# Two token blocks' last-phase work placed in TensorE's fixed order

## The chip, the cores and the metric

The kernel runs on one core of a Trainium2 chip. The core has TensorE (PE in the profile; the loads of its stationary operand are a row of their own, PEld), VectorE (DVE), ScalarE (ACT), GpSimd (POOL) and SyncE (SP), which here only issues DMAs. The metric is device time in microseconds (us), the median of several runs. Before the change it is 2971.01 us (three runs, 2964.57 to 2972.19).

## The reference

A decoder block over 2048 tokens of width 1024, in float32, with two mixers side by side; cut to its core:

```python
def _rwkv7_scan(r, decay, k, v, kk, b):
...
    def step(state, inp):
        r_t, w_t, k_t, v_t, kk_t, b_t = inp
        sk = jnp.einsum('bhvk,bhk->bhv', state, kk_t)
        state = (state * w_t[:, :, None, :] - sk[..., None] * b_t[:, :, None, :]
                 + v_t[..., None] * k_t[:, :, None, :])
        return state, jnp.einsum('bhvk,bhk->bhv', state, r_t)
...
def _conv_branch(val, gate, og, conv_k, conv_b, ln_g, ln_b, w_o):
    u = val * jax.nn.sigmoid(gate)
    u = _causal_depthwise_conv(u, conv_k, conv_b)
    u = _layernorm(u, ln_g, ln_b, LN_EPS)
    u = jax.nn.silu(u) * jax.nn.silu(og)
    return u @ w_o
...
        h = _rmsnorm(x, norm_g[l]) * (1.0 + scale[:, None, :]) + shift[:, None, :]
        p = jnp.einsum('bsd,de->bse', h, w_in[l])
        c_val, c_gate, c_og, ts, r_og, g_conv, g_rwkv = jnp.split(p, SPLITS, axis=-1)
...
        m = jax.nn.sigmoid(g_conv) * y_conv + jax.nn.sigmoid(g_rwkv) * y_rwkv
        out = jnp.einsum('bsd,de->bse', m, w_out[l])
        x = x + gate[:, None, :] * out
    return _rmsnorm(x, final_g)
```

The second mixer normalises the scan's output by head, adds a bonus term, gates it and multiplies it by w_rwkv_out. Its recurrence is the only part in which tokens depend on each other in a long row.

## The kernel before, in words

**Tiling.** Tokens go in four blocks of 512 (`TB`), b = 0 to 3; channels in eight tiles of 128 (`KT`). Every float32 product is made as three products of rounded parts (hi by hi, lo by hi, hi by lo; `mm3k`, L314), so a 128-channel output tile of a block takes 8 x 3 products of 512 columns. `msplit` cuts each in two of 256 columns in the first phase and leaves it at 512 in the last.

**First phase.** For each block 73 tiles of the input projection are made: K, R and V for the recurrence, value and gate for the convolution, one low-rank tile and four kinds of gates. Results that the last phase needs go to HBM: `o_d` (recurrence), `bv_d` (its bonus), `ro_d`, `co_d` (gates of the two mixers), `gr_d`, `gc_d` (merge gates), `y_d` (convolution). The recurrence is done in 16 groups G = 4b + g of four heads: `pair` (L582 on) makes chunk operands, `inverse` inverts a triangular matrix on GpSimd (31 dependent steps of two operations, L754 and L758), `merge` completes it on TensorE (L806, L816), and `group` walks a chain of eight steps of three small products each (L858, L864, L871), with a DVE operation between each two, then two products for the output (L885), a normalisation, and two transposes (L920) whose results are stored as `o_d`. Chain G needs chain G-1's end, and the K tiles of group G wait for chain G-2.

**TensorE's fixed order.** In the first phase the order on TensorE is written out by a small simulation, `compose`. Its clock counts only planned TensorE time (`te`). Threads (the steps of pair, group, inverse and merge, and background work) say after how much planned time they go on; between them jobs (a projected tile each, in pieces of one k) fill in. `pick` takes the first of the next `LOOK` = 13 jobs whose condition holds. `swap` exchanges the block's input tiles (`h_hi`, `h_lo`, eight buffers each) for those of the next block, which `hprep` loads and splits; `duo` interleaves two jobs so that the eight input tiles come free, or are first needed, one after the other. The other engines' orders and the DMA queue are made by a scheduler that knows priorities and data; each engine then runs its list in order. `behind` ties an operation to a place in TensorE's order.

**Background.** In blocks 1 and 2 a thread (`side`) splits the weights of the last phase into hi and lo and stores them, one item after another. In block 3 `z_thread` makes block 0's inputs for the last phase: `z_first` (o + bv) x ro, stored as `z_d`, and `lnorm_first`, the layer norm of `y_d` with its swish and gate, stored as `u_d`.

**Last phase.** After the fixed order is closed (`ctx_pe.__exit__`), for each block: `rproj` (eight tiles of w_rwkv_out, into `mr`), `cproj` (eight of w_conv_out, merged and split into `m_hi`, `m_lo`), the output product with w_out (`pout`, L1402 to L1404, 4 column blocks), the residual sum (L1410), the last RMS norm and the store (L1423). Block 0 takes `z_d` and `u_d` by `lsplit`. For the next block `osplit` (L1273, L1274 and the splits at L1251, L1252) and `lnorm` make the inputs while the output product runs. Their tiles lie where the first phase's lay: a pool can be used as soon as the tiles that were in its place are no longer needed. Block 0's tiles lie on the right side of the memory (`oa`), the next blocks' also on the left, where the chain's tiles were (`late`).

## Time and profile before

| what | us |
|---|---|
| median of three runs | 2971.01 |
| the profiled execution, device time | 2974.13 |
| its span (first to last record) | 2972.3 |
| span, until the first phase's projections end | about 2324 |
| span, the first output product begins | 2433.4 |
| span, the last product of the last chain (L885) begins | 2473.2 |

The profile is of one execution. Its page gives busy time by engine, the span in 40 slices, the chain of work that ended last, and groups of instructions by line of the kernel; the trace also answers for windows of time, for single tiles, for waits by engine and for lists of instructions in order of time. "Idle before <- releaser" names what the engine waited for last. The mean granted clock of TensorE was 0.974 over the span.

### The profile page before, as it was taken

The page shows a single profiled execution, that of the slowest core. Times are in us where ns is not written, and L with a number is a line of the kernel's source. Part 1 is how long each engine was busy: PE and PEld are TensorE (multiplying, and loading weights), DVE is VectorE, ACT ScalarE, POOL GpSimd, SP SyncE. Part 2 cuts the span into 40 slices and gives each one's busy share as a digit, 9 for nine tenths or more (in the row PEclk, how much of TensorE's full clock was granted, in tenths as well). Part 3 has the DMA queues.
Part 4 walks back from the last instruction along what each step waited for, and adds up shares of the span by engine and source line. Part 5 has one row for each costly group of instructions (what it writes and reads, how often), then busy time and mean ns, then how long its engine had stood idle before and what let it go on. Part 6 is the DMA issues. An engine that isn't in the chain of part 4 may idle for free.

```text
span 2972.3 us, 64197 instructions
## 1 busy us (share of the span) xinstructions
PE 2787.3 (94%) x25672; PEld 2625.0 (88%) x25672; DVE 2014.0 (68%) x3867; ACT 939.1 (32%) x1779; POOL 1273.5 (43%) x1790
## 2 busy tenths in 40 slices
PE   6998999899999999999999999999999995899998
PEld 6888989899999998999999889989999784687988
DVE  6695876767677685868595758686877443767333
ACT  4443334333333323332233232323333222333201
POOL 2456535742534352435334445466463424646000
PEclk9999999999999999999999999999999997999999
DMA  8776866766767675867667677666665765979684
GB/s 315 268 251 220 276 224 241 250 210 209 240 225 229 205 247 185 273 219 240 201 208 219 210 239 253 210 200 232 202 225 175 240 245 170 364 251 345 240 288 166
DMA packets 361548, 699.18 MB, mean 235 GB/s; under 512 B 129121, under 2 KB 147873, under 8 KB 361250
## 3 DMA queue, kind: packets, MB, share of 16 engines
q1 hardware_dynamic: 361250, 695.08, 69.6%
q8 instruction: 202, 3.31, 0.5%
q14 instruction: 96, 0.79, 0.1%
HBM read 506.14 MB, written 187.70 MB: 233 GB/s over the span
## 4 chain that ended last, share of the span: by engine, by line
PE 54%; DVE 18%; DMA 4%; issue 2%; POOL 1%; ACT 1%; SPq 0%; DVEq 0%; POOLq 0%; ACTq 0%
PE ps_main L314 40%; DVE acc L972 5%; PE xo L864 2%; PE xo L858 1%; PE xo L871 1%; PE pout L1402 1%; PE pout L1404 1%; PE pout L1403 1%; DVE uv L891 1%; PE aux L674 1%; DMA ct<-co_d 1%; DVE T L776 1%; DVE As L677 1%; DVE As L821 1%; DVE gst L910 1%
## 5 line engine op out<-in xcount | busy, mean ns | idle before, releaser
L314 PE MATMUL ps_main<-h_hi,w_hi 128*128 128x256 f32 x4608 | 968.0, 292 | 26.0 <-issue 13.8
L314 PE MATMUL ps_main<-h_hi,w_lo 128*128 128x256 f32 x4608 | 911.8, 280 | 3.5 <-POOL w_lo L293 3.0
L314 PE MATMUL ps_main<-h_lo,w_hi 128*128 128x256 f32 x4608 | 912.5, 280 | 0.0
L314 PEld LDWEIGHTS ps_main<-h_hi,w_hi 128*128 128x128 f32 x4608 | 708.6, 191 | 51.8 <-issue 16.5
L314 PEld LDWEIGHTS ps_main<-h_hi,w_lo 128*128 128x128 f32 x4608 | 706.1, 190 | 4.1 <-POOL w_lo L293 3.4
L972 DVE SCALAR_TENSOR_TENSOR acc<-u,ck,acc 128x512 f32<-128x512 f32 x928 | 696.7, 751 | 19.1
L314 PEld LDWEIGHTS ps_main<-h_lo,w_hi 128*128 128x128 f32 x4608 | 708.7, 190 | 0.0
L758 POOL TENSOR_TENSOR TT<-TT,itmp 128x126 f32<-128x126 f32 (+22 forms) x496 | 198.1, 399 | 35.4
L754 POOL TENSOR_TENSOR itmp<-La,TT 128x126 f32<-128x126 f32 (+22 forms) x496 | 187.7, 378 | 55.9 <-DMA La<-dA 21.0
L293 POOL TENSOR_TENSOR w_lo<-w_st,w_hi 128x1024 fp32r<-128x1024 f32 x51 | 123.7, 2426 | 183.8 <-ACT w_hi L291 157.0
L853 ACT ACTIVATE Se<-S,pe 128x128 f32<-128x128 f32 x256 | 89.0, 395 | 313.3 <-DVE S L875 311.8
L875 DVE TENSOR_TENSOR S<-xo,Se 64x128 f32<-64x128 f32 x256 | 73.6, 287 | 137.5 <-PE xo L871 133.0
L866 DVE TENSOR_TENSOR uv<-xo,rn 64x256 f32<-64x256 f32 x128 | 53.8, 421 | 126.6 <-PE xo L864 125.3
L291 ACT CAST w_hi<-w_st 128x1024 fp32r<-128x1024 f32 x71 | 74.5, 1050 | 193.7 <-DMA w_st<-w_in_t 158.6
L642 POOL TENSOR_TENSOR ta<-ta,k 128x512 f32<-128x512 f32 x32 | 45.1, 1411 | 176.5 <-ACT ta L641 176.5
L557 ACT ACTIVATE t<-ps_main,mu 128x512 f32<-128x512 f32 x96 | 65.8, 685 | 133.1 <-PE ps_main L314 130.9
L677 DVE TENSOR_TENSOR As<-aux,maskA 128x512 f32<-128x512 f32 x128 | 82.8, 684 | 31.8 <-PE aux L674 31.4
L687 POOL TENSOR_TENSOR BK<-BK,pe 128x1024 f32<-128x1024 f32 x32 | 63.5, 1984 | 95.2 <-PE aux L674 82.7
L864 PE MATMUL xo<-XO,As 64*64 64x64 f32 x1024 | 88.1, 227 | 12.4 <-DVE XO L860 12.4
L864 PEld LDWEIGHTS xo<-XO,As 64*64 64x64 f32 x1024 | 70.3, 137 | 32.8 <-DVE XO L860 16.1
L674 PE MATMUL aux<-KR,BK 64*128 64x128 f32 x1024 | 83.2, 291 | 15.7 <-DVE As L677 7.1
L860 DVE TENSOR_TENSOR XO<-xo,XO 128x256 f32<-128x256 f32 x128 | 53.5, 418 | 58.9 <-PE xo L858 58.3
(303 smaller groups left out, 5267.2 us busy)
## 6 DMA issues: line engine op xcount, KB each, us to landing
w_hi<-kh_in SPq DMA_DIRECT2D x219, 512.0 KB, 5.2
w_lo<-kl_in SPq DMA_DIRECT2D x219, 512.0 KB, 3.9
w_st<-w_in_t SPq DMA_DIRECT2D x73, 512.0 KB, 4.7
kh_in<-w_hi SPq DMA_DIRECT2D x71, 512.0 KB, 2.8
kl_in<-w_lo SPq DMA_DIRECT2D x71, 512.0 KB, 4.1
w_hi<-kh_ro SPq DMA_DIRECT2D x32, 512.0 KB, 6.0
w_lo<-kl_ro SPq DMA_DIRECT2D x32, 512.0 KB, 5.7
w_hi<-kh_co SPq DMA_DIRECT2D x32, 512.0 KB, 5.5
```

The costliest lines, as they stand in the source:

```text
L291: nc.scalar.copy(hi, st)
L293: lo_eng.tensor_tensor(out=lo, in0=st, in1=hi.bitcast(F32), op=ALU.subtract)
L314: lastpe[0] = te(0.113 * 2 / ms).matmul(ps[:, qs], ww[:, k, :], aa[k][:, qs], start=(k == 0 and t == 0 and q == 0), stop=(k == KT - 1 and ...
L557: nc.scalar.activation(t1, ps, AF.Identity, scale=mu1[:, mi:mi + 1])
L674: te(0.166).matmul(pA[hh][:, c // 2, es], BK[hs, cc, es], KR[hs, cc, es], start=(c == 0), stop=(c == 3), skip_group_check=True)
L677: nc.vector.tensor_tensor(out=Asb[:, hh, c4 * 4:c4 * 4 + 4, :].rearrange("p (a e) n -> p a (e n)", e=2), in0=pA[hh], in1=flat(maskA).unsqu ...
L754: first = nc.gpsimd.tensor_tensor(out=tmp[:, :ni, :nt], in0=La[:, j:j + 1, j + 1:].broadcast_to([P, ni, nt]), in1=TT[:, :ni, j:j + 1].broa ...
L758: nc.gpsimd.tensor_tensor(out=TT[:, :ni, j + 1:], in0=TT[:, :ni, j + 1:], in1=tmp[:, :ni, :nt], op=ALU.add)
L853: nc.scalar.mul(Se[:, q, :], Sg[:, q, :], R[q]["pe"][:, c:c + 1])
L864: te(0.155).matmul(xo[pr_, q, hs], As[q][pr_, hh, c, kcol(e)], XO[pr_, c, q, hs], start=(q == 0 and hh == 0), stop=(q == 1 and hh == 1), s ...
L875: nc.vector.tensor_tensor(out=Sg[hs, :, hs], in0=xo[hs, 2:4, hs], in1=Se[hs, :, hs], op=ALU.add)
L972: nc.vector.scalar_tensor_tensor(out=acc if i + 1 < HALO else yj, in0=u[:, i:i + TB], scalar=ck[:, j, i:i + 1], in1=acc, op0=ALU.mult, op1 ...
```

## The change

Blocks 0 and 1 (`NPB` = 2) get their last-phase projections and output products inside TensorE's fixed order. `rjob`, `cjob` and `ojob` do there what `rproj`, `cproj` and the output loop do, with `z_d` and `u_d` of the block brought in as TensorE's input tiles by `hprep` and `swap`; their results lie in buffers of the first phase that are free by then (the tiles of pair, the small pool `xp`, `h_lo`, and for block 0 an `As` buffer). Block 3's fill jobs (convolution and gates) are put behind all its K, R and V tiles, `LOOK` becomes 80 there, and the last chain keeps the same planned step as the others (3.4 instead of 2.8). The background makes block 1's inputs as well as block 0's, both before the fixed order needs them: `side` runs two threads side by side on the weights, then `z_first` and `lnorm_first` for block 0 and block 1, each with its loads one or two tiles ahead; it rests while a block's own inputs are being made (`free`), and those wait while one of its items is under way (`blk["s"]`). Behind the fixed order the last phase begins with block 2, and its pools are laid out anew: block 2's tiles lie on the left (`hl`, `b2`), block 3's on the right.

```diff
 LOOK, DUO, NHF, LHF, LYJ = 13, 2, 9, 5.0, 34.0
+LOOK3, LSD = 80, 2.6
+NPB = 2
...
-        for n, j_ in enumerate(jobs[:LOOK]):
+        for n, j_ in enumerate(jobs[:look[0]]):
...
-            if starts and jobs.index(starts[0][1]) < NHF and ("x", starts[0][0]) in done:
+            if starts and "next" not in blk and (starts[0][1] not in jobs or jobs.index(starts[0][1]) < starts[0][2]) and ("x", starts[0][0]) in done:
...
+        if b < NB:
+            src = [xT_dram[b][:, k, :] for k in range(KT)]
+        else:
+            src = (u_dram if (b - NB) % 2 else z_dram)[(b - NB) // 2]
         hf = []
+        yield (lambda: not blk.get("s"), 0.0)
...
+            behind(nc.sync.dma_start(hf[k], src[k]))
...
     def last(G, a, b):
-        return b if G == NB * len(groups) - 1 else a
+        return a
...
-    def product(ti, take, dve=0):
+    def product(ti, take, dve=0, name="in"):
         wcount[0] = dve
-        w = load_w("in", ti)
+        w = load_w(name, ti)
...
         if part == 0:
-            ys, n_ = yload(0), yload(1)
+            yield (free, 1.0)
...
+                item(1)
+                behind(nc.gpsimd.tensor_tensor(out=ys, in0=ys, in1=n_.pop(0), op=ALU.add))
+                if j + 2 < KT:
+                    n_.append(yload(j + 2))
+                yield LSD
+                item(-1)
             ln0["ys"] = ys
         elif part == 1:
+            n_ = [yload(0), yload(1)]
...
             yield (late_free, 0.0)
             ps = pl.tile([P, TB], F32, name="late", tag="late")
...
-                yield LLD
+                yield (free, 0.0)
+                item(1)
+                yj = n_.pop(0)
                 behind(nc.gpsimd.tensor_tensor(out=yj, in0=yj, in1=ln0["mean"], op=ALU.subtract))
                 yield 1.5
                 behind(nc.scalar.activation(yj, yj, AF.Square))
+                if j + 2 < KT:
+                    n_.append(yload(j + 2))
+                yield 1.5
                 if j == 0:
                     qs = yj
                 else:
-                    nc.gpsimd.tensor_tensor(out=qs, in0=qs, in1=yj, op=ALU.add)
+                    behind(nc.gpsimd.tensor_tensor(out=qs, in0=qs, in1=yj, op=ALU.add))
+                yield LSD / 2
...
+    def z_first(pb):
+        def load(j):
+            r = hx("z"), hx("zb"), hx("zr")
+            for t_, d_ in zip(r, (o_dram, bv_dram, ro_dram)):
...
+        for j in range(KT):
+            yield (free, 0.0)
+            item(1)
+            z, bt, rt = n_.pop(0)
+            if j + 1 < KT:
+                n_.append(load(j + 1))
             behind(nc.gpsimd.tensor_tensor(out=z, in0=z, in1=bt, op=ALU.add))
             nc.gpsimd.tensor_tensor(out=z, in0=z, in1=rt, op=ALU.mult)
             yield 2 * LST
-            behind(nc.sync.dma_start(z_dram[j], z))
+            behind(nc.sync.dma_start(z_dram[pb][j], z))
+            item(-1)
 
...
+    def free():
+        return not blk.get("x") and "next" not in blk
+
+    def item(d):
+        blk["s"] = blk.get("s", 0) + d
+
+    def worker(work):
+        while work:
+            yield (free, 1.0)
+            if work:
+                item(1)
+                yield from work.pop(0)()
+                item(-1)
 
     def side():
         work = []
         for g in groups:
             work += [lambda n_=n_, half=half: keep(*n_, half) for n_ in pending[4 * g:4 * g + 4] for half in range(2)]
-            work.append(lambda g=g: gate_cols(g))
-        work += [lambda n_=n_, half=half: ogate(n_, half) for n_ in later for half in range(2)]
-        for w in work:
-            yield (lambda: not blk.get("x"), 1.0)
-            yield from w()
+        other = Thread(worker(work), 3, 0)
+        yield 7.0
+        yield from worker(work)
+        yield (lambda: other not in threads, 1.0)
+        for g in groups:
+            yield (free, 1.0)
+            item(1)
+            yield from gate_cols(g)
+            item(-1)
+        work = [lambda n_=n_, half=half: ogate(n_, half) for n_ in later for half in range(2)]
+        other = Thread(worker(work), 3, 0)
+        yield 7.0
+        yield from worker(work)
+        yield (lambda: other not in threads, 1.0)
+        for pb in range(NPB):
+            yield (lambda pb=pb: ("norm", 4 * pb + 3) in done, 2 * LST)
+            yield from z_first(pb)
+            done.add(("x", NB + 2 * pb))
+            for i in range(3):
+                yield from lnorm_first(pb, i)
+            done.add(("x", NB + 2 * pb + 1))
 
     def start_pairs(b, g):
...
+    def rjob(b, n):
+        def take(ppr):
+            mr0 = w4.setdefault(("mr", b), [])
+            mr0.append(e1.tile([P, TB], F32, name="mr0", tag=mtags[n]))
+            with tc.high_priority(HP):
+                nc.vector.scalar_tensor_tensor(out=mr0[n], in0=w4.pop(("th", n)), scalar=1.0, in1=ppr, op0=ALU.add, op1=ALU.mult)
+
+        def run():
+            w4["th", n] = th = e2.tile([P, TB], F32, name="rth0", tag="t2", bufs=T2B)
+            nc.sync.dma_start(th, gr_dram[b][n])
+            yield from product(n, take, -1000, "ro")
...
+    def cjob(b, n):
+        def take(ppc):
+            mr0, m0 = w4["mr", b], w4.setdefault(("m", b), ([], []))
+            th = w4.pop(("th", n))
+            with tc.high_priority(HP):
+                nc.vector.scalar_tensor_tensor(out=th, in0=th, scalar=1.0, in1=ppc, op0=ALU.add, op1=ALU.mult)
+            nc.vector.scalar_tensor_tensor(out=mr0[n], in0=th, scalar=0.25, in1=mr0[n], op0=ALU.mult, op1=ALU.add)
+            hi = (xp.tile([P, TB], F32R, name="m_hi0", tag="hx") if n < HXB else
...
+            nc.scalar.copy(hi, mr0[n])
+            nc.vector.tensor_tensor(out=lo, in0=mr0[n], in1=hi.bitcast(F32), op=ALU.subtract)
+            m0[0].append(hi)
+            m0[1].append(lo)
...
+    def xload(b):
+        w4["x", b] = xts0 = []
+        for half in range(2):
+            for tt in range(NTT):
+                xt = e1.tile([P, TB], F32, name="xt0", tag=mtags[4 * half + tt])
+                nc.sync.dma_start(xt, x[b * TB + tt * P:b * TB + tt * P + P, half * TB:half * TB + TB])
+                xts0.append(xt)
+        w4["small", b] = e2.tile([P, HALO + TB], F32, name="small0", tag="u")
+
+    def ojob(b, cb):
+        m0, xts0 = w4["m", b], w4["x", b]
+        ws = [[flat(t_).rearrange("p (k n) -> p k n", n=256) for t_ in load_w("o", (cb, kh))] for kh in range(2)]
+        if cb == 3:
+            w4["fg"] = flat(whl.tile([P, KT, P], F32, name="fg0", tag="w", bufs=WB))
+            nc.sync.dma_start(w4["fg"], final_g.unsqueeze(0).broadcast_to([P, D]))
+        yield 1
...
+        for kh in range(2):
+            whi, wlo = ws[kh]
+            for tt in range(NTT):
+                ts_ = slice(tt * P, tt * P + P)
+                o_ = pts[tt // 2][:, tt % 2, :]
+                for k in range(4):
+                    kk = kh * 4 + k
+                    st_ = kk == 0 and tt % 2 == 0
+                    te(0.113).matmul(o_, m0[0][kk][:, ts_], whi[:, k, :], start=st_, stop=False, skip_group_check=True)
+                    te(0.113).matmul(o_, m0[0][kk][:, ts_], wlo[:, k, :], start=False, stop=False, skip_group_check=True)
+                    lastpe[0] = te(0.113).matmul(o_, m0[1][kk][:, ts_], whi[:, k, :], start=False, stop=(kk == KT - 1),
+                                                 skip_group_check=True).ins
+                    if k % 2 and not (kh and k == 3 and tt == NTT - 1):
+                        yield 1
...
+        for tt in range(NTT):
+            xt = xts0[4 * (cb // 2) + tt][:, (cb % 2) * 256:(cb % 2) * 256 + 256]
+            with tc.high_priority(HP):
+                nc.vector.tensor_tensor(out=xt, in0=pts[tt // 2][:, tt % 2, :], in1=xt, op=ALU.add)
+            sq = e2.tile([P, TB], F32, name="fsq0", tag="t2", bufs=T2B)[:, :256]
+            nc.scalar.activation(sq, xt, AF.Square, accum_out=sq4[:, tt, cb:cb + 1])
+        if cb == 3:
+            vs, rs, rt = sm[:, 16:20], sm[:, 20:24], sm[:, 24:28]
+            nc.vector.tensor_reduce(out=vs, in_=sq4, axis=AX.X, op=ALU.add)
+            nc.vector.tensor_scalar(out=vs, in0=vs, scalar1=1.0 / D, scalar2=RMS_EPS, op0=ALU.mult, op1=ALU.add)
...
+                    nc.vector.scalar_tensor_tensor(out=xt, in0=xt, scalar=rs[:, tt:tt + 1], in1=w4["fg"][:, hs],
+                                                   op0=ALU.mult, op1=ALU.mult)
+                    nc.sync.dma_start(out[b * TB + tt * P:b * TB + tt * P + P, hs], xt)
...
             seg = steer(*plan)
+            if b + 1 == NB and g == 0:
+                jobs.append(mark(lambda: look.__setitem__(0, LOOK3)))
+            if b + 1 == NB and phase2:
+                rest += seg[len(seg) - len(f):]
+                seg = seg[:len(seg) - len(f)]
             if g == 3 and b + 1 < NB:
                 seg[-2:] = [[None, duo(seg[-2], seg[-1]), 0]]
-                starts.append((b + 1, seg[-1]))
+                starts.append((b + 1, seg[-1], NHF))
             jobs += seg
+    if phase2:
+        last_ = rest
+        last_[-2:] = [[None, duo(last_[-2], last_[-1]), 0]]
+        jobs += last_
+        for pb in range(NPB):
+            i_ = NB + 2 * pb
+            starts.append((i_, last_[-1], NHF if not pb else 4))
+            rp, cp = [rjob(pb, n) for n in range(KT)], [cjob(pb, n) for n in range(KT)]
+            rp[-2:] = [[None, duo(rp[-2], rp[-1]), 0]]
+            if pb + 1 == NPB:
+                cp[-2:] = [[None, duo(cp[-2], cp[-1]), 0]]
+            starts.append((i_ + 1, rp[-1], NHF))
+            jobs += [mark(swap, 2, lambda i_=i_: ("h", i_) in done and ("B", 1) in flagd[G]), [None, duo(rp[0], rp[1]), 0]] + rp[2:]
+            jobs += [mark(swap, 2, lambda i_=i_: ("h", i_ + 1) in done and ("x", NB + 2 * NPB - 1) in done), [None, duo(cp[0], cp[1]), 0]] + cp[2:]
+            last_ = [[None, ojob(pb, cb), 0] for cb in range(4)]
+            jobs += [mark(lambda pb=pb: xload(pb), 2, None)] + last_
...
 
     wcount[0] = -1000
     msplit[0] = MS2
-    mr = mnew()
-    rproj(0, lsplit(z_dram), mr)
-    cproj(0, lsplit(u_dram), None)
-    mhi, mlo = okt(0, MOFF)
...
-    for b in range(NB):
-        if b:
-            mhi, mlo = okt(b, MOFF)
-            cproj(b, uhl, (mhi, mlo))
+    ohl = osplit(NPB)
+    uhl = lnorm(NPB)
+    mr = mnew()
+    rproj(NPB, ohl, mr)
+    fg = hx2.tile([P, D], F32, name="fg", tag="fg", bufs=1)
+    nc.sync.dma_start(fg, final_g.unsqueeze(0).broadcast_to([P, D]))
+    for b in range(NPB, NB):
+        mhi, mlo = okt(b, MOFF)
+        cproj(b, uhl, (mhi, mlo))
         if b + 1 < NB:
             ohl = osplit(b + 1)
             uhl = lnorm(b + 1)
```

## What the change should do to the time

> **What bounds the kernel now.** First the page's head and its slices, to see which engine is full and where it isn't.
>
> ```profile
> span 2972.3 us, 64197 instructions
> PE 2787.3 (94%) x25672; PEld 2625.0 (88%) x25672; DVE 2014.0 (68%) x3867; ACT 939.1 (32%) x1779; POOL 1273.5 (43%) x1790
> PE   6998999899999999999999999999999995899998
> PEclk9999999999999999999999999999999997999999
> ```
>
> TensorE (PE) is full in nearly every slice but two near the end (5 and 8), and there the granted clock dips too (7). So the second view is the windows, cut at the kernel's stages: blocks 1, 2 and 3 of the first phase, then block 0's projections, then the stretch from block 0's first output product to block 1's, then the rest.
>
> ```profile
> 618.00:1182.00 564.00, 554.17 (x5685) 534.43 (x5686) 412.83 (x814) 182.32 (x357) 229.20 (x394) 1.00 0.69 222
> 1182.00:1751.00 569.00, 551.34 (x5629) 531.41 (x5626) 408.17 (x812) 181.15 (x356) 242.80 (x405) 0.99 0.69 222
> 1751.00:2324.00 573.00, 551.06 (x5582) 528.88 (x5582) 416.08 (x758) 173.69 (x316) 301.36 (x446) 0.98 0.66 216
> 2324.00:2433.00 109.00, 108.91 (x747) 89.23 (x748) 52.17 (x101) 22.68 (x43) 41.33 (x72) 0.97 0.78 268
> 2433.00:2644.00 211.00, 161.02 (x948) 135.76 (x947) 114.52 (x219) 55.78 (x112) 99.86 (x70) 0.88 0.73 262
> 2644.00:2830.00 186.00, 181.24 (x1167) 162.96 (x1166) 110.23 (x227) 63.45 (x135) 56.79 (x38) 1.00 0.76 274
> ```
>
> Columns: the stretch, its length, busy time of PE, weight loads, DVE, ACT, POOL, then granted clock, DMA share, GB/s. In the blocks PE is busy 96 to 98%: nothing that only moves work between other engines can gain there. In 2433 to 2644 it is busy 161 of 211 us, at a clock of 0.88. The third view, what PE waits for in that stretch, names the largest holes:
>
> ```profile
> PE pout L1402 <- DVE xt L1410: 19.7, 3, 17.9
> PE late L920 <- POOL uv L913: 11.4, 1, 11.4
> ```
>
> Both lie around the last chain's end: PE has run out of block 0's work, block 1's inputs can only be made once the first phase's memory is free, and PE stands. This hole is what the change can win, and I see no other.
>
> **The size of the hole.** What must PE do between the first output product of block 0 and that of block 1? The starts are in the answer for the tile pout, the pace of block 3's two projections and the pieces of the chain in the chain of waits and the timeline:
>
> ```profile
> L1402 PE MATMUL pout<-w_hi,o_hi x256: 276/281/684, 2433.4 to 2829.2; 128*128 128x256 f32 x128
> L1402 PE MATMUL pout<-w_hi,m_hi x256: 276/281/684, 2643.6 to 2961.5; 128*128 128x256 f32 x128
> 2829.70 87.06 PE ps_main L314 x384
> 2434.98 0.61 PE L858 MATMUL xo<-S,KR 128*128 128x128 f32 x4
> 2438.25 0.68 PE L864 MATMUL xo<-XO,As 64*64 64x64 f32 x8
> 2469.72 1.93 PE late L885 x32
> 2486.53 1.13 PE late L920 x4
> 2650.89 0.86 PE prl L1359 x2
> ```
>
> Projections of a block: 87.1 us. Output product: block 3's runs from 2829.70 + 87.06 = 2916.8 to 2961.5, 45 us. The chain's rest: a step has three groups like the two shown, 0.61, 0.68 and again about 0.61, so 1.9 us, and five are left, 9.5; two products of L885, 3.9; two transposes, 2.3; three small products of the normalisation, about 2.5: 18 us. Sum 45 + 87 + 18 = 150, and the stretch took 2643.6 - 2433.4 = 210. So **60 us are lost**. The windows say the same in another way: 50 us not busy, and 161 busy us for 150 us of work at a clock of 0.88.
>
> **The change, part by part.**
>
> *Work that only moves.* The loop's matmuls for blocks 0 and 1 (two projections and an output product each, 132 us of PE a block) go from behind the fixed order into it. Their number of columns is the same. The projections become 256 wide, twice as many, where they were 512 wide:
>
> ```profile
> 2196.68 4.10 PE ps_main L314 x36
> ```
>
> 4.10/36 = 113.9 ns; two are 227.8 ns against 87.06/384 = 226.7: 1.1 ns by 768 wide products, 1 us more. [...]
>
> *What fills the hole.* From 2324 the order holds block 0's and 1's work and the chains' rest: the 109 us that PE filled to 2433, the 150 us above, and block 1's output product, 45: 304 us, less the normalisation that goes, so it ends near 2325. + 302 = 2626 if nothing stalls. When does the last chain end? The chains are paced by their own latency, two groups at a time:
>
> ```profile
> 1958.33 1.15 PE L885 MATMUL late<-uv,As 128*64 128x64 f32 x32
> 2238.81 1.15 PE L885 MATMUL late<-uv,As 128*64 128x64 f32 x32
> 2473.21 1.99 PE late L885 x32
> ```
>
> Groups 11 and 13 end 280 us apart with fill beside them; group 15 came 234 later since PE was emptying and its step was planned at 2.8 us, not 3.4. With full fill it ends at 2238.8 + 280 = 2519 and, with the 17 us that lie between the last product and the last transpose (2473 to 2489), its outputs are out near 2540. That is 85 us before the order ends, and in those 85 us, plus the 44 us of block 2's first projection, block 2's inputs are made. Before, block 1's needed from 2490 to 2603 with the DMA at its limit:
>
> ```profile
> DMA packets 10042, 23.06 MB, mean 384 GB/s; under 512 B 1112, under 2 KB 1112, under 8 KB 10037
> ```
>
> (23.06 MB between 2540 and 2600.) 113 us needed against 85 + 44 = 129: it fits, with 16 us to spare. So I count the hole as closed: -60.
>
> *Four exchanges of PE's input tiles* (swap) come in. Three follow directly on work that reads the same eight buffers, as the blocks' starts do today; the fourth falls behind an output product that doesn't read them. At the starts of blocks 1 to 3 the timeline has
>
> ```profile
> 614.31 0.77 PE L314 MATMUL ps_main<-h_hi,w_hi 128*128 128x256 f32 x2 [3.13 <-issue]
> 1189.39 0.50 PE L314 MATMUL ps_main<-h_hi,w_hi 128*128 128x256 f32 x2 [1.57 <-ACT th L959]
> 1764.17 0.47 PE L314 MATMUL ps_main<-h_hi,w_hi 128*128 128x256 f32 x2 [1.48 <-ACT th L959]
> ```
>
> (in brackets the idle time), mean 2.1: three times, +6. Bounds 0 and, at the largest, four times 3.1, 12.
>
> *Making the inputs.* Removed behind the loop: 16 reloads with their splits (block 0), 40 loads, 38 POOL products and the splits of block 1. Added inside: 32 reloads with splits, and for block 1 62 POOL operations, 56 loads and 16 stores; block 0's 62 move from block 3 to block 2. Splits sit on DVE and ACT, 73 and 30% busy in block 3 (416 and 174 of 573): covered. The DMA share is 0.66 there: covered. POOL is not free, since the triangular inverse of each group is a row of 62 dependent POOL operations on the chain's path:
>
> ```profile
> 1478.73 0.24 POOL L754 TENSOR_TENSOR itmp<-La,TT 128x31 f32<-128x31 f32 x1 [0.28 <-DMA La<-dA]
> 1510.33 0.25 POOL L758 TENSOR_TENSOR TT<-TT,itmp 128x16 f32<-128x16 f32 x1
> 1764.51 0.24 POOL L754 TENSOR_TENSOR itmp<-La,TT 128x31 f32<-128x31 f32 x1 [0.84 <-DMA La<-dA]
> 1815.70 0.25 POOL L758 TENSOR_TENSOR TT<-TT,itmp 128x16 f32<-128x16 f32 x1
> 1831.44 1.20 PE L806 MATMUL late<-T,As 32*32 32x32 f32 x64 [0.51 <-DVE uv L891]
> ```
>
> Undisturbed it takes 32 us (1478.7 to 1510.6), beside two background threads 51 (1764.5 to 1816.0); still PE, which uses it next at 1831, waited only 0.5. So 20 us of lateness are hidden. The new background is denser (a step each 2.6 to 9 us of planned time, where it was 8 to 17) and may hold one or two inverses up by a further few us: +5, bounds 0 and 75 (rival 3).
>
> *SyncE's queue.* The new loads of gates and of x, the reloads and the stores stand in one queue with the weights, which already blocks:
>
> ```profile
> SPq L285 <- PE ps_main L314: 487.6, 114, 14.2
> w_hi<-kh_ro SPq DMA_DIRECT2D x32, 512.0 KB, 6.0
> ```
>
> Between 1180 and 2324 it waited 114 times for a free weight buffer (4.3 us each), that is, it runs ahead of PE, with three pairs of 5.5 us against 6.0 us to land. final_g takes one of the seven buffers in each block's last output product; two pairs in front still cover 6 us. I cost it at 0; if the cover goes, a load late by 6 us, once a block, 12.
>
> *The hand-over.* Block 2's products are written where block 1's x tiles lay, free only when block 1's rows are stored: the last addition, 8 scalings and a store behind PE's last product, against two products of 5.5 us that go on meanwhile. +4, bounds 0 and 15.
>
> **Sum.** -60 + 1 + 6 + 5 + 0 + 4 = -44, from the profiled execution's own 2974.1 (span 2972.3): 2930. The median of the runs shown is 3.1 below that execution, so **2927**.
>
> **Rivals.** *1: the hole moves to the hand-over.* DVE takes its instructions in order, and one that waits for a load holds back the evacuations behind it. That made the 17.9 us hole:
>
> ```profile
> 2505.24 1.08 DVE L1252 TENSOR_TENSOR m_lo<-ot,m_hi 128x512 fp32r<-128x512 f32 x1 [11.76 <-ACT m_hi L1251]
> 2506.36 1.42 DVE L1410 TENSOR_TENSOR xt<-pout,xt 128x256 f32<-128x256 f32 x4
> ```
>
> The addition PE needed stood behind a subtraction that waited 11.8 us for block 1's data. [...] Here the data has 16 us to spare, so I hold it for the lesser case. If it recurs once: 2927 + 18 = 2945; with a slow refill behind it, up to 2957. *2: nothing moves.* The fixed order ends before the last chain, so the same wait follows. It needs the chain 85 us later than 2540; the rows above give no reason. 2962 to 2980. *3: slower.* POOL's inverses. With 20 us hidden, lateness costs from the 21st us on. The inverse's own work and one background operation, in block 3 by lines:
>
> ```profile
> L758 POOL TENSOR_TENSOR TT<-TT,itmp 128x126 f32<-128x126 f32 (+22 forms) x125 | 49.9, 399 | 8.5
> L754 POOL TENSOR_TENSOR itmp<-La,TT 128x126 f32<-128x126 f32 (+22 forms) x126 | 47.7, 379 | 17.5 <-DMA La<-dA 9.2
> L1026 POOL TENSOR_TENSOR lny<-lny 128x512 f32<-128x512 f32 x8 | 11.7, 1465 | 0.1
> ```
>
> 31 by 399 and 31 by 379 ns are 24 us. The densest background step has two operations of that kind, 2.9 us, in 4.3 of plan; beside it the inverse would take 24 x 4.3/1.4, about 74, so 15 to 20 beyond what is hidden. Five inverses (of the eight in blocks 2 and 3): 75 instead of 5, so 2997. It turns the sign from the fourth on. Against it: higher priority of the chain, and that each phase lasts only some tens of us.
>
> **How the numbers follow.** Forecast 0.60 (2905 to 2936), rival 1 0.22 (2936 to 2957), rival 2 0.08, rival 3 0.10. 2905 is every new cost at zero and some us of the small holes after 2644 gone too. Range 2905 to 2958, which leaves out rivals 2 and 3. A measurement here tells about 0.3%, 9 us, from no change: faster 0.82, within 0.08, slower 0.10.
>
> **What would show it.** The slices' 5 and 8 gone and the clock at 0.97 or more to the end; PE's fixed order ending near 2626 and the last chain's last transpose near 2540; block 2's first projection starting within 10 us of it; blocks 1 to 3 within 10 us of 564 to 573. Wrong if PE has a hole over 15 us behind 2500, if an inverse takes over 55 us with PE idle before L806's successor, or if block 3 ends with PE standing.

## The result, and the profile after

The changed kernel takes 2930.5 us (median of four runs, 2926.0 to 2934.5) against 2971.6 for the kernel before, measured beside it: ratio 0.9864, 95% interval 0.984 to 0.9887. The forecast was 2927. The profiled execution has a span of 2928.8 us, 43.5 less than before.

The head and the slices of its page, as of before (busy tenths of PE, then the granted clock in tenths):

```profile
span 2928.8 us, 65806 instructions
PE 2774.6 (95%) x26432; PEld 2651.2 (91%) x26432; DVE 2016.7 (69%) x3775; ACT 937.3 (32%) x1779; POOL 1301.1 (44%) x1814
PE   6999999899999999999999989999999999998998
PEclk9999999999999999999999999999999999999999
```

The slices' 5 and 8 are gone. To see where the time went, both spans are cut at the same events: the start of each block (the tanh of its low-rank tile on ACT) and the first output product of blocks 0, 1 and 2, which the answer for the tile pout gives (first and last start stand behind the three durations; L1323 is the output product inside the fixed order, blocks 0 and 1, L1578 that of block 2):

```profile
L1323 PE MATMUL pout<-w_hi,m_hi x256: 276/279/553, 2426.0 to 2631.8; 128*128 128x256 f32 x128
L1578 PE MATMUL pout<-w_hi,m_hi x128: 276/276/363, 2739.9 to 2784.1; 128*128 128x256 f32 x128
```

The table has two executions of each kernel: those of the first profiles, and one more each from the experiments below.

| stretch | before | before, again | after | after, again |
|---|---|---|---|---|
| block 0 | 574.8 | 578.7 | 567.3 | 570.6 |
| block 1 | 563.8 | 566.7 | 560.2 | 560.4 |
| block 2 | 569.5 | 569.9 | 569.6 | 568.3 |
| block 3's start to block 0's output product | 669.4 | 669.5 | 674.0 | 672.1 |
| to block 1's output product | 210.2 | 210.4 | 149.9 | 149.1 |
| to block 2's output product | 140.7 | 142.7 | 164.0 | 164.0 |
| to the end | 188.0 | 188.0 | 188.9 | 188.8 |

So the hole of 60 us is closed to the microsecond (210.2 to 149.9), some 23 us come back in the next stretch (140.7 to 164.0), and of the rest most is block 0, 7.5 us shorter. The windows of the three stretches from 2426 on (length, busy PE, weight loads, DVE, ACT, POOL, granted clock, DMA share, GB/s):

```profile
2426.00:2576.00 150.00, 147.76 (x1323) 145.53 (x1322) 65.16 (x127) 28.00 (x70) 15.47 (x10) 1.00 0.76 269
2576.00:2632.00 56.00, 50.52 (x387) 48.56 (x388) 23.71 (x34) 16.28 (x45) 33.51 (x25) 0.91 0.92 336
2632.00:2740.00 108.00, 93.25 (x407) 75.97 (x406) 73.77 (x107) 31.80 (x52) 53.69 (x36) 0.94 0.88 317
...
2632.00:2660.00 28.00, 13.96 (x63) 11.05 (x62) 27.43 (x47) 12.37 (x21) 18.74 (x12) 0.82 0.95 318
```

In the first PE is busy 148 of 150 us at full clock. The second is block 1's output product: 45 us of work in 56. The third is block 2's two projections: 87 us of work in 108, and the last row is its beginning, where DVE is busy 27.4 of 28 us. What PE waited for in these two:

```profile
PE ps_main L316 <- DVE mr L1480: 14.0, 1, 14.0
PE pout L1323 <- DVE cth L1272: 2.6, 2, 2.1
PE pmean L1508 <- POOL ys L1506: 2.5, 1, 2.5
```

(mr and cth are the evacuations of products with w_rwkv_out and w_conv_out; ys is the sum, made on POOL, of which pmean's product makes the mean of block 2's layer norm.) Idle time explains 14.7 of the 21 us lost in the third stretch and 5.5 of the 11 in the second. Counted by line, the layer norms' own products (pmean, pvar, prl), which are not in the 87 and the 45, take 2.8 and 2.1 us more. The last 2.9 and 3.6 us are the projections and the output product themselves, which run slower behind a wait, and this is most of it: from 2658.8 to 2663.3 the products of 512 columns start 0.43 us apart, and 0.23 once that is over. The first row is the evacuation of block 2's first product, mr(0). DVE's timeline shows why it came only at 2658 (L1344 are block 1's eight final scalings; L326, L1540 and L1432 belong to block 2's layer norm), and POOL's what ran beside it:

```profile
2638.61 9.53 DVE L1344 SCALAR_TENSOR_TENSOR xt<-xt,small,fg 128x512 f32<-128x512 f32 x8
2648.06 1.75 DVE L326 SCALAR_TENSOR_TENSOR y<-th,y 128x512 f32<-128x512 f32 x1
2649.84 1.63 DVE L1540 TENSOR_TENSOR y<-y,ct 128x512 f32<-128x512 f32 x1
...
2656.42 1.75 DVE L326 SCALAR_TENSOR_TENSOR y<-th,y 128x512 f32<-128x512 f32 x1
2658.10 1.27 DVE L1480 SCALAR_TENSOR_TENSOR mr<-rth,ps_main 128x512 f32<-128x512 f32 x2
2659.29 0.68 DVE L326 SCALAR_TENSOR_TENSOR y<-th,y 128x512 f32<-128x512 f32 x1
```

```profile
2642.76 13.19 POOL L1538 TENSOR_TENSOR y<-y,rl 128x512 f32<-128x512 f32 x8 [0.22 <-ACT rl L1532]
```

Block 2's first product began at 2632.8, right behind the order, and the second was done near 2645. From there PE had no free accumulator for 14.0 us. DVE never stood still: it worked off the scalings and six layer-norm operations that its list has ahead of mr(0). And it worked slowly: 1.63 to 1.75 us an operation while POOL ran its row of eight, 0.68 for the same operation once POOL was through.

### The profile page after: what moved, and what is told of

Its sections match the earlier page's. It is cut to its first block, busy times and chain, and to the rows that moved or that the text cites. A ratio compares the mean times of both kernels' runs of the same rounds, so it can differ in the third digit from the quotient of the medians.

```text
span 2928.8 us, 65806 instructions
## 1 busy us (share of the span) xinstructions
PE 2774.6 (95%) x26432; PEld 2651.2 (91%) x26432; DVE 2016.7 (69%) x3775; ACT 937.3 (32%) x1779; POOL 1301.1 (44%) x1814
## 4 chain that ended last, share of the span: by engine, by line
PE 53%; DVE 15%; POOL 5%; DMA 4%; issue 2%; ACT 1%; SPq 0%; DVEq 0%; POOLq 0%; ACTq 0%
PE ps_main L316 38%; DVE acc L982 5%; PE xo L874 2%; PE xo L881 1%; PE xo L868 1%; POOL itmp L764 1%; POOL TT L768 1%; PE aux L684 1%; PE pout L1580 1%; PE pout L1578 1%; PE pout L1579 1%; PE pout L1323 1%; PE pout L1325 1%; PE pout L1324 1%; DMA As<-dT 1%
## 5 line engine op out<-in xcount | busy, mean ns | idle before, releaser
L316 PE MATMUL ps_main<-h_hi,w_hi 128*128 128x256 f32 x5120 | 1069.8, 291 | 27.6 <-issue 15.1
L316 PE MATMUL ps_main<-h_hi,w_lo 128*128 128x256 f32 x5120 | 1010.3, 279 | 3.5 <-DMA w_lo<-kl_co 1.7
L316 PE MATMUL ps_main<-h_lo,w_hi 128*128 128x256 f32 x5120 | 1011.9, 279 | 0.0
L316 PEld LDWEIGHTS ps_main<-h_hi,w_hi 128*128 128x128 f32 x5120 | 784.7, 190 | 55.0 <-issue 18.3
L316 PEld LDWEIGHTS ps_main<-h_hi,w_lo 128*128 128x128 f32 x5120 | 781.9, 190 | 4.5 <-DMA w_lo<-kl_co 2.1
L316 PEld LDWEIGHTS ps_main<-h_lo,w_hi 128*128 128x128 f32 x5120 | 785.4, 190 | 0.0
L764 POOL TENSOR_TENSOR itmp<-La,TT 128x126 f32<-128x126 f32 (+22 forms) x496 | 188.8, 381 | 74.4 <-DMA La<-dA 40.7
L718 POOL TENSOR_TENSOR vv<-rk,vv 128x512 f32<-128x512 f32 x32 | 42.0, 1314 | 136.0 <-ACT rk L717 122.8
```

The costliest lines, as they stand in the source:

```text
L316: lastpe[0] = te(0.113 * 2 / ms).matmul(ps[:, qs], ww[:, k, :], aa[k][:, qs], start=(k == 0 and t == 0 and q == 0), stop=(k == KT - 1 and ...
L764: first = nc.gpsimd.tensor_tensor(out=tmp[:, :ni, :nt], in0=La[:, j:j + 1, j + 1:].broadcast_to([P, ni, nt]), in1=TT[:, :ni, j:j + 1].broa ...
```

## The experiments

Three questions: is the gain cover for the last chain, as the prediction has it; what holds mr(0) up; and where do the other differences come from?

**Only block 0 in the order (e_one).**

```diff
-NPB = 2
+NPB = 1
...
-        if b % 2 == 0:
+        if (b - NPB) % 2 == 0:
```

(The second line only keeps the last phase's tile sets alternating.)

> Only block 0's projections and output products stand in the fixed order; block 1's inputs are made behind it again. Theory 1 (the gain is cover: two blocks of products, 260 us, beside the last chains and the first inputs behind the order; with one block the inputs, 113 us, have 45 us of output products beside them): a hole of 40-70 us on PE returns near 2500-2560, time 2955-2985, little or nothing gained against before. Rival (the gain comes from standing in the order and from the background at all): at most 15 us above the changed kernel's, 2930-2945.

Measured: 2965.8 us, ratio to before 0.9977 (0.9965 to 0.9988). The hole is back, at 2460 to 2545, 85 us with 38 busy and the clock at 0.57; its two windows are

```profile
2460.00:2500.00 40.00, 12.52 (x111) 9.92 (x109) 18.70 (x51) 4.89 (x12) 3.80 (x2) 0.56 0.51 171
2500.00:2545.00 45.00, 25.25 (x49) 13.13 (x50) 13.39 (x16) 9.53 (x16) 41.84 (x32) 0.58 0.70 235
```

One block's products in the order win 9 us by the medians of that session, two win 41. What counts is how much work lies beside the last chain and ahead of the first inputs made behind the order. Theory 1.

**mr elsewhere (e_mr).** A set of tiles is taken from the same pool ahead of mr, so that mr's eight tiles lie in another place (by the order of the pool; the trace prints no addresses). DVE's list stays.

```diff
+    okt(NPB + 1)
     ohl = osplit(NPB)
     uhl = lnorm(NPB)
```

> The tiles mr lie elsewhere in the memory (another set is taken ahead of them), and DVE's list is that of the changed kernel. Theory 1 (the list holds mr(0) up): mr(0) again 13-16 us behind the second product, idle PE 12-16 us. Theory 2, the prediction's (mr, or the products' tiles, wait for block 1's x tiles to be stored): the hole moves or shrinks to below 8 us.

Measured: one run, 2934.4 us; the wait for mr(0) is 13.9 us. Moving the tile changes nothing: theory 1, against the prediction's.

**The second half of the layer norm behind mr(1) (e_ln).** `after_` makes its first instruction wait for its second, `mrs` collects the evacuations, and `half` is called between the layer norm's halves.

```diff
-        nc.scalar.copy(rl, flat(prl))
+        half()
+        cp = nc.scalar.copy(rl, flat(prl))
+        if b == NPB:
+            after_(cp, mrs[1])
...
-    uhl = lnorm(NPB)
     mr = mnew()
-    rproj(NPB, ohl, mr)
+    uhl = lnorm(NPB, lambda: rproj(NPB, ohl, mr, (0, 1)))
+    rproj(NPB, ohl, mr, range(2, KT))
```

> The second half of block 2's layer normalisation (from the copy of rl on) waits for mr(1), so that DVE's list has mr(0) and mr(1) straight behind block 1's eight final scalings, and POOL's eight multiplications by rl start behind mr(1). Theory 1 (the hole at the hand-over is DVE's list: six layer-norm operations of 10 us in all ahead of mr(0)): mr(0) moves from 2658 to about 2648, the hole of 14.0 us shrinks to 3-4, and the time falls by about 10 us against the changed kernel's, to about 2920. Theory 2, the prediction's (the tile that mr(0) or the first products need comes free only when block 1's rows are stored, 2639-2648 and landing later): mr(0) stays near 2658, the time stays at 2930 +- 3. Rival 3: the delayed normalisation is late for block 2's conv-out products and a hole opens near 2720-2740, time 2930-2945.

Measured: 2931.8 us, ratio 0.9861 (0.9833 to 0.9889), no gain. DVE's timeline has mr(0) and mr(1) right behind the scalings, 12.8 us after block 1's last output product (2629.0) where it was 26.3, and then mr(2) behind the same kind of row:

```profile
2635.47 6.43 DVE L1344 SCALAR_TENSOR_TENSOR xt<-xt,small,fg 128x512 f32<-128x512 f32 x8
2641.83 1.27 DVE L1480 SCALAR_TENSOR_TENSOR mr<-rth,ps_main 128x512 f32<-128x512 f32 x2
...
2661.67 1.75 DVE L326 SCALAR_TENSOR_TENSOR y<-th,y 128x512 f32<-128x512 f32 x1
2663.34 0.68 DVE L1480 SCALAR_TENSOR_TENSOR mr<-rth,ps_main 128x512 f32<-128x512 f32 x1
```

Nothing but DVE's list had held mr(0): here it is written as the scalings end, before the store of block 1's last row is even issued (2643.3). Together with e_mr, that rules theory 2 out. But the price moved along: PE now waits 10.3 us for mr(2). Theory 1's place was right and its gain wrong.

**Dealt out among the eight products (e_spread).** Each item's multiplication by rl waits for one more mr:

```diff
+        if step:
+            step(0)
         for j in range(KT):
+            if step and j + 1 < KT:
+                step(j + 1)
...
-            EN[LE].tensor_tensor(out=y[j], in0=y[j], in1=rl, op=ALU.mult)
+            ym = EN[LE].tensor_tensor(out=y[j], in0=y[j], in1=rl, op=ALU.mult)
+            if step:
+                tc.add_manual_dep(ym.ins, mrs[-1].ins.name, ...)
```

> Block 2's layer normalisation is dealt out among its eight ro products: the multiplication by rl of item j, on POOL, waits for mr(j+1), so DVE's list never has more than three of its operations ahead of an mr, and POOL never runs a row of eight. In the run that only put the second half behind mr(1), mr(0) and mr(1) came at once (2641.8 us) and the wait went to mr(2), behind six layer-norm operations of 1.3 to 1.75 us (10.3 us of idle PE). Theory 1 (DVE's list, and POOL beside it, set the hole wherever the operations lie): no idle stretch above 4 us between 2630 and 2740, 8-12 us less than the changed kernel's, 2919-2923. Rival: the last items come too late for block 2's first co product, 5-15 us of idle PE near 2725, 2925-2935. Rival 2, the prediction's (storing block 1's rows holds a tile that the products need): a wait of 10-14 us stays near 2650-2665.

Measured: 2936.7 us, ratio 0.9877 (0.9857 to 0.9897). No wait is above 2.9 us, and still PE stands some 12 us in all between 2640 and 2700, in eight pieces, part of them at ACT's and DVE's last splits of u and o. The hole is spread as thin as the work was.

**The multiplication on DVE (e_le).**

```diff
-OE, LE, CE = 0, 0, 1
+OE, LE, CE = 0, 1, 1
```

> The multiplication by rl goes from POOL to DVE for blocks 2 and 3: DVE's list has 14 layer-norm operations in place of 6 ahead of mr(0), and POOL is idle then. Theory 1 (an operation with two SBUF inputs takes 1.75 us beside POOL's row and 0.68 without it): the final scalings take 6 us, not 9.5, the 14 operations 0.6-0.7 us each, 9-10 us in all, and mr(0) comes at 2653-2656, earlier than 2658 in spite of eight more operations; PE idle 9-12 us. Theory 2 (these operations are slow by themselves just there, by DMA or by their place): 14 operations of 1.7 us and 9.5 us of scalings, mr(0) near 2672, PE idle 27 us, about 2943.

Measured: 2931.6 us, ratio 0.986 (0.9844 to 0.9876). On DVE's timeline, with POOL idle from 2645.4 to 2653.6, and POOL's next operation:

```profile
2641.54 6.42 DVE L1344 SCALAR_TENSOR_TENSOR xt<-xt,small,fg 128x512 f32<-128x512 f32 x8
2647.88 4.90 DVE L1538 TENSOR_TENSOR y<-y,rl 128x512 f32<-128x512 f32 x8
...
2655.70 0.68 DVE L326 SCALAR_TENSOR_TENSOR y<-th,y 128x512 f32<-128x512 f32 x1
2656.30 1.76 DVE L1432 TENSOR_TENSOR u_lo<-y,u_hi 128x512 fp32r<-128x512 f32 x1
2657.99 1.27 DVE L1480 SCALAR_TENSOR_TENSOR mr<-rth,ps_main 128x512 f32<-128x512 f32 x2
```

```profile
2653.62 3.90 POOL L1456 TENSOR_TENSOR ot<-ot,rt 128x512 f32<-128x512 f32 x1 [8.21 <-DMA rt<-ro_d]
```

The scalings take 6.4 us, not 9.5, and the layer-norm operations 0.6 to 0.7 each, except the last, 1.76. Beside DVE's row it is now POOL's single operation that is long: 3.90 us instead of 1.29. Counted from the last output product of block 1 (2634.9 here, 2631.8 in the changed kernel), mr(0) comes after 23.1 us instead of 26.3, with eight operations more ahead of it, and PE waits 10.9 us. Theory 1: the slowness is POOL's neighbourhood.

**Moved ahead of the hand-over (e_hp3, e_hp4).** In the changed kernel one of block 2's four variance products runs at 2603.8 and three only at 2632, behind the order, so everything after them falls on DVE's busiest time. e_hp3 gives that part a high priority and puts the splits of u behind mr(1) to mr(4), and block 3's mean behind a product of block 2. Core of the edit:

```diff
-        pvar = pa.tile([P, NTT], F32, name="pvar", tag="pvar")
+        with tc.high_priority(HP) if b == NPB else ExitStack():
+            pvar = pa.tile([P, NTT], F32, name="pvar", tag="pvar")
...
+            for hi, lo, src in late_y[2 * n - 2:2 * n] if b == NPB and n else []:
+                nc.scalar.copy(hi, src)
```

> The variance part of block 2's layer normalisation (pvar, rsqrt, dg, prl, copy of rl) gets a high priority, so that its four pvar products follow one another near 2604 and not one near 2604 and three behind the fixed order (2632), and its multiplications run beside block 1's output products, where DVE was busy 8 of 32 us. The splits of u are put behind mr(1) to mr(4) and block 3's pmean behind block 2's second co product. Four arrangements of the same DVE work behind 2632 (changed kernel 14.0 us, half behind mr(1) 10.3 + 4, dealt out 12, on DVE alone 11 + 2) left 10-14 us of idle PE each. Theory 1 (DVE has too much to do between 2632 and 2680, wherever it stands; only moving it ahead of 2632 helps): idle PE 0-3 us between 2630 and 2740, 10-12 us less than the changed kernel's, about 2920. Theory 2 (a constant wait of the hand-over, not DVE's: stores, tiles, loads of rth): 10-14 us of idle PE remain, 2930.

Measured: 2928.9 us, ratio 0.9838 (0.9819 to 0.9857). From block 1's last output product to block 2's first the stretch shrinks from 108.1 to 99.6 us, and in its first 28 us DVE is busy 16.1 us instead of 27.4, PE 23.3 instead of 14.0:

```profile
2639.00:2667.00 28.00, 23.30 (x99) 18.85 (x98) 16.13 (x30) 6.73 (x15) 9.93 (x8) 0.94 1.04 405
```

PE still waits 8.1 us there for DVE (6.9 for mr), between the two theories' 0 to 3 and 10 to 14. Moving part of DVE's work ahead took away 6.6 of the 14.7 us of idle time, so its amount was part of the limit; how much of the rest it makes isn't shown. And block 1's output product itself, with that work beside it, now takes 58.0 us instead of 55.9, and the stretch ahead of it 154.0 instead of 149.9. One row shows the next thing in line, a load:

```profile
2640.35 0.69 DVE L1553 TENSOR_TENSOR y<-y,ct 128x512 f32<-128x512 f32 x1 [2.55 <-DMA ct<-co_d]
```

Net, pout of block 0 to pout of block 2 takes 311.6 us against 313.9. e_hp4 adds a guard for block 2's mean:

```diff
+            w4.setdefault(("p", b), lastpe[0])
...
-        if b > NPB:
-            tc.add_manual_dep(mm.ins, w4["c", b - 1].name,
+        tc.add_manual_dep(mm.ins, (w4["c", b - 1] if b > NPB else w4["p", NPB - 1]).name,
```

> As the run before, and block 2's pmean product stands behind the first half of block 1's first column block, so that its eight subtractions follow the last cth in DVE's list. Theory 1: of the 5.5 us of idle PE near 2580, 2.5 on ys and 1-2 on cth go; 2-4 us less than the run before, about 2917, if the layer norm, now 5 us later, still ends ahead of 2632. Rival: what goes at 2580 comes back at 2640, same time as the run before.

Measured: 2933.3 us, 0.9857 (0.9833 to 0.9881), again 311.6 from pout to pout. The idle time near 2580 falls to 2.6 us, and two other waits come up:

```profile
PE ps_main L316 <- DMA w_lo<-kl_ro: 6.8, 1, 6.8
PE pvar L1531 <- POOL qs L1527: 3.3, 1, 3.3
```

The rival: what goes at 2580 comes back. By their ratios e_hp3 and e_ln2 (below) are the fastest kernels here, but both intervals overlap the changed kernel's.

**The mean behind the column block (e_ln2).** As e_ln, with pmean behind block 1's first column block.

```diff
+            w4.setdefault(("p", b), lastpe[0])
...
+            tc.add_manual_dep(mm.ins, w4["p", NPB - 1].name, ...)
```

> As the run before, and block 2's pmean product also stands behind the output products of block 1's first column block instead of among them. Theory 1 (pmean's two subtractions stand ahead of the last cth in DVE's list and cost the smaller hole): the 24 us stretch from 2576 loses its 5.5 us of idle time and runs at a clock above 0.9, another 5-8 us fall away, to about 2913. Rival: PE waits there for the last cth and its split in any case, the hole stays at 4-8 us and the time is that of the run before +- 2. Second rival: the layer norm starts 50 us later and is late for block 2's conv-out products; a hole of 10-30 us near 2730, 2930-2950.

Measured: 2926.5 us, ratio 0.9845 (0.982 to 0.9871). Block 1's output product takes 50.8 us instead of 55.9, so pmean and its subtractions did cost 5 there; the stretch ahead of it is 2.0 longer and the waits for mr add up to 9.8. From pout to pout 309.8, the best of all, 4 us below the changed kernel, which this measurement can't tell from none.

**The chain's old spacing (e_last).**

```diff
     def last(G, a, b):
-        return a
+        return b if G == NB * len(groups) - 1 else a
```

> One part of the change undone: the last group's chain is issued by the old, shorter spacing. In the changed kernel PE has work beside the chain either way, so what counts is whether the chain's end, 2551, holds anything up. Theory 1 (the fixed order is bound by PE's work, 95% busy): time within 4 us of the changed kernel's, 2926-2934, although the last transposes come 10-20 us earlier. Rival (the order's tail still waits for the chain): 8-14 us faster, 2917-2922. Second rival (the tight chain stalls PE again, as in the profile of before): 5-15 us slower.

Measured: 2934.3 us, ratio 0.9864 (0.9839 to 0.9889). Counted from block 3's start the last chain's last product comes 14 us earlier (748.6 instead of 762.5), and the order's last output product 3 us later (883.1 instead of 879.8). The chain's end holds nothing up any more: theory 1. The microseconds only change places: the stretch from block 0's output product to block 1's takes 160.7 us instead of 149.9, and the next one 150.4 instead of 164.0, though nothing was changed at the hand-over.

**Once more, and the places in HBM (rep_after, rep_before, e_lay).** The first two are unchanged copies. e_lay is the kernel before with the changed kernel's scratch tensors:

```diff
-    z_dram = [dp.tile([P, TB], F32, name=f"z_d{j}", tag=f"z_d{j}") for j in range(KT)]
-    u_dram = [dp.tile([P, TB], F32, name=f"u_d{j}", tag=f"u_d{j}") for j in range(KT)]
+    z_dram, u_dram = [[[dp.tile([P, TB], F32, name=f"{n}{b}_{j}", tag=f"{n}{b}_{j}") for j in range(KT)] for b in range(2)][0]
+                      for n in ("z_d", "u_d")]
```

> The changed kernel once more, for a second profile. Block 1 starts at 630.7 us in the profile of before and at 622.2 in that of after, although every engine's list is the same in both up to about there. Theory A (it is variation from run to run): the second profile starts block 1 anywhere in 620-632 and the span moves by as much, 2925-2938. Theory B (the change does it, by where tensors lie in HBM): block 1 starts at 622 +- 1 again and the span is 2929 +- 2. The hole at the hand-over, 14.0 us from about 2645 to 2659, and the smaller one of 9 us near 2580 are there again in both.

> The kernel before once more, for a second profile. Theory A (block 0's length varies from run to run; the changed order has given 622.2, 626.6, 623.9, 626.0, 629.7 for block 1's start over five profiles with the same lists up to there, before 630.7): block 1 starts anywhere in 622-632. Theory B (the old kernel is slower in block 0): 630-631 again. From block 1's start to the end of the span before took 2341.6 us, and 2301-2307 in the changed kernel's two profiles and its close relatives: 2338-2345 again, and the idle stretch of PE behind 2433 is there again with 60 us +- 6.

> The kernel before, with the two sets of scratch tensors z_d and u_d in HBM that the changed kernel has; the added set isn't used, so only the places of the tensors behind it differ. Every engine's list is that of before. Block 0 took 574.8 and 578.7 us in before's two profiles and 566.6 to 573.8 in ten of the changed order, with the same lists up to block 1's start. Theory A (chance): anything from 567 to 579. Theory B (the places in HBM do it): 567-572, and 5 us less than before in all, about 2967 beside 2973. Theory C (something else of the changed program, its length or its tiles' places on the chip): 574-579 and no gain. One profile can only rule out B or C, not A.

Measured: 2931.1, 2983.7 (one run) and 2974.5 us (ratio to before 0.9998, 0.9989 to 1.0008). The two holes and their causes repeat: 13.9 us for mr(0) in the copy of after, 210.4 us from pout to pout in that of before. The places in HBM aren't what shortens block 0: e_lay took 574.0 us for it, as before. In all, block 0 took 574.0 to 578.7 us in three profiles of the old program and 567.0 to 573.8 in ten of the changed one and its relatives (e_one: 575.6), though every engine's list is the same up to 622 us. It may be real, some 5 us, but three profiles against eleven whose ranges touch don't settle it, and its cause is open; so is that of the 4 to 5 us in block 1, where the background's lists do differ.

## Why the prediction was right, and where it wasn't

The sum was -44 and the profiles differ by -43.5 (the medians by -41). Term by term it is less good than that.

- **The hole, -60: right.** From block 0's output product to block 1's, 150 us were forecast from the work and 149.9 were measured; e_one shows the cover to be the cause. The agreement to 0.1 us has luck in it: the chain's rest took 12.0 us, not 18, and projections, output product and idle time took 89.6 + 46.1 + 2.2, not 87 + 45. The times that went into it held: the order ended at 2632 (forecast 2626), the last transposes came near 2550 (2540).
- **The hand-over, +4, bounds 0 and 15: mis-sized, and its mechanism wrong.** It is +23 (140.7 to 164.0). The prediction named the tiles where block 1's x lay, "free only when block 1's rows are stored". e_mr and e_ln show that no tile held mr(0): DVE's list did, with eight scalings and six layer-norm operations ahead of it. The prediction's "113 us needed against 85 + 44 = 129" counted when the inputs are complete, and so they were: no wait above 1 us stands behind 2660. What it left out is that making them shares DVE with evacuating PE, busy 98% of those 28 us, and that POOL's part of them makes DVE's operations some 2.6 times as long (1.75 for 0.68).
- **Rival 1** came near to this: an evacuation held back in DVE's list by an operation whose data is late, 18 us and up to 30 with a slow refill. Just so it occurred once, and small: DVE stood 3.3 us for pmean's product, the last cth waited behind pmean's subtractions, and PE waited 2.1. At mr(0) the place was the rival's and the reason wasn't: no data was late there, DVE was at work all the time. The slow refill cost 2.9 and 3.6 us. The rival was given 0.22; the time it gave, 2945, didn't come since other terms were too dear.
- **Swaps +6, background on POOL +5, width +1: too dear.** At the usual pace the width costs nothing: in the projections most products of 256 columns start 113.3 ns apart in the timeline and most of those of 512 columns 226.7, so two such narrow ones take as long as a wide one. From block 2's start to block 0's output product, where the background and two of the four swaps lie, the difference is +4.7 in the first pair of profiles and +1.0 in the second. Behind 2324 the swaps show in no wait above 1.3 us. The inverse that starts at 1755.6 took 49.6 us, the longest behind block 0, and as long as before (51.4); PE's waits between block 1's end and 2330 that could come of a late inverse are

```profile
PE late L826 <- DVE Qs L820: 5.6, 5, 1.6
PE late L816 <- DVE T L786: 1.8, 2, 1.4
```

  5.6 and 1.8 us in all, 3.6 and 0.7 before. Rival 3 (75 us) didn't occur.
- **Block 0 and 1, 0: wrong.** They give 7.5 and 3.6 us; the prediction had no term for them.
- **What would show it.** The slices came as written, and so did blocks 1 to 3: 560 and 570 us, and for block 3, from its start to the first evacuation of block 0's projections, 578 where it was 575. Block 2's first projection started at 2632.8, right behind the order. "the clock at 0.97 or more to the end" didn't hold: 0.91 and 0.94 in the two stretches. The hole behind 2500 stayed 1 us below the 15 that would have counted as wrong.

So the time was right because a term 19 us too small met terms some 8 too dear and some 11 us that no term named. The closed hole is understood; the agreement of the sum to 0.5 us is luck.

**What stays open** is why six arrangements of the hand-over all end within 4.1 us of each other: from block 3's start to the end of the span the changed kernel takes 1176.8 and 1174.0 us, its relatives with two blocks in the order 1172.7 to 1175.5. PE's waits between 2560 and 2745 fell from 22.0 us to 18.5 in e_hp3 and 15.6 in e_hp4, and the time from block 0's output product to block 2's by only 2.3. In both, block 1's output product is longer (58.0 and 58.9 us instead of 55.9) and waits for weights come up, 4.1 and 6.8 us. A slower clock it isn't: over that stretch it is 0.98 and 0.97, and 0.96 in the changed kernel. The DMA share between 2560 and 2740 is 0.91 in the changed kernel and in e_hp4; that points to the transfers of block 2's and 3's inputs beside the weights. No run took those loads away, so it isn't shown.

## What to carry to other kernels

Here the work put beside the last chain was worth the whole hole, 60 us counted and 210.2 to 149.9 measured: count what must run and how long the chain takes, and the size of the hole follows. At the place where one mode of working hands over to the next, ask not only when the inputs are ready but which engine makes them and what else is in its list: mr(0) stood behind eight scalings and six layer-norm operations of DVE, and PE waited 14.0 us for it. And when a wait is removed and the time stays, look for the same microseconds at the next product before calling the theory wrong.

## What the runs showed of the hardware

An operation of DVE on 128 x 512 floats with both inputs in the on-chip memory takes 0.61 us in a row (4.90 for eight in e_le, with POOL idle) and 1.63 to 1.75 beside a row of POOL operations; POOL's own go from 1.29 to 1.65 (13.19 for eight). DVE's subtractions of pmean, which have one of their inputs in an accumulator, stay short beside POOL: in the changed kernel six take 3.67 us from 2585.36 on, and of POOL's sums for qs, from 2585.58 on, the first three take 1.29 us each. When DVE's splits follow (two from 2590.07 on, both inputs in the on-chip memory, 1.77 us each), the next three of those sums take 1.61. So both sides show it; in e_le it is POOL's operation that takes 3.90 us. Beside POOL's row of eight DVE's operations start 1.67 us apart, less than 0.61 + 1.29 = 1.90, so part of the two still overlaps. Why the two lengthen each other isn't shown.

The holes cost more than their idle time here. The 28 us around the 14.0 us wait have a granted clock of 0.82, and behind the wait the products start 0.43 us apart for 4.5 us before they are back at 0.23: some 2.2 us on top. After two short waits it was the same: behind 2.5 and 2.1 us near 2580, with only pmean's product between them, the products of 256 columns start 0.21 us apart from 2585.6 to 2591.5, and 0.12 after that.
